# Layer 0's input projection in batches of four row blocks, with wider convolution taps

## The chip, the cores and the metric

The kernel runs on one core of a Trainium2 chip. The metric is the device time of one launch in microseconds (us); lower is better. The engines are named as in the profile: PE (TensorE, matrix products), ACT (ScalarE), DVE (VectorE), POOL (GpSimd), SP (SyncE, which issues the DMAs).

## The reference

A two-layer encoder over 256 tokens of width 2048, all in float32. Each layer first computes a modulation from a conditioning vector c and then one wide input projection, whose columns feed four kinds of mixers; an output projection with a gate and a gated feed-forward follow. What the change touches, for layer 0:

```python
mod = silu(c) @ w_mod + b_mod              # shift, scale, gate, ...: 2048 wide each
h = layernorm(x) * (1 + scale) + shift     # (256, 2048)
p = h @ w_in                               # one product, then cut by columns
a, g = p[:, AG]        # 1024 columns: GLU a * sigmoid(g), then a causal depthwise
                       # convolution of 31 taps over the tokens, norm, silu
u, v = p[:, UV]        # 512 + 512: gated MLP over tokens; v = gelu, normalised, mixed
q_lat, kv_lat, kr = p[:, B]   # 704: low-rank attention
sc = p[:, SC]          # 1024: short convolutions
gate = p[:, SB]        # 512: gate of that mixer
x = x + mod_gate * (concat(four mixers) @ w_out)
```

## The kernel before, in words

Tokens stay in SBUF; weights (and the modulation's weights) stream through once. `hF` holds the normalised x transposed: 16 row blocks ("kt") of 128 channels by 256 tokens, in four tiles. A *block* of PE work is one kt of 128 output columns: two float32 passes of 128x256 by the profile's count.

**Modulation.** For layer 0, `mod_block` (profile line L190) loads one 128x2048 piece of w_mod (1 MiB, tile `wmod`) and reduces it against c on DVE to one column. Two such pieces (shift, scale) make `first_mod_of(...).block(kt)`, which adds the bias (L1398) and modulates `hF[kt]`: on ACT for even kt (L116), on DVE for odd (L1404). Pieces for later stages, of L190 or of the accumulating form L200, are interleaved with the weights of B, C, and the output projection, so many MiB per load step as the table `RATES` says.

**The input projection of layer 0** is `by_pieces`. Its column groups are D (the GLU's 1024), U, V and E (u, v and gate; 512 each), then B (704) and C (1024). D accumulates in four PSUM banks over all 16 kt. U, V and E take turns in two banks each: the kt are cut into pieces `PIECES` of 1, 1, 2, 4, 4 and 4, and each piece's partial product is copied out by ACT (L1234, L1239) and added to a sum in SBUF by DVE (L1240). Within a piece a quarter of D's turns alternates with U, V and E.

For kt below `PLAIN_KT` = 4, and for U, V, E, B, C everywhere, products are plain float32 (weights in tile `wexact`, issued at L368). For D from kt 4 on, the weight (tile `wraw`, L373) is split: ACT rounds it (`whi`, L384), DVE subtracts (`wlo`, L385), `hF` is split in the same manner into `hT` (L403, L404), and PE makes three products of rounded operands in place of one plain product. Lines L113 and L116 are the helpers through which all products and all ACT activations go.

**Buffers.** `wraw` and `wmod` share four buffers of 1 MiB; `wexact` has eight of 512 KB, that it shares with `whi` and `wlo`. SP issues loads in the order of the code, and waits where a buffer is not free. `mods_for` decides how many modulation pieces are issued before a weight load: those that its kt needs, and further ones while the planner's PE clock is more than `LEAD_US` ahead of its DMA clock.

**After it.** `mix_d` makes the GLU and queues the convolution (`convD`, L824: one DVE operation for each of 31 taps and 4 column blocks) as background work, of which B and C run so many pieces after each load step as `STEPS` says. `mix_u`, `gelu_v` and `mix_v` finish u and v; `latent_group` makes B's latents; `group` makes C while `attend` interleaves attention's products (`ps_q`, `ps_kr`, `ps_qn`, `ps_kn`, `ps_v`, `ps_sc`, `ps_pT`, `ps_o`), whose results come out through ACT (`qg`, `rope`, `qn`, `kn`, `vv`, `p`) and DVE. `ps_mix` is the product that mixes the v tokens. The output projection follows (products `o`): its first chunk is 1024 columns in three rounded products, its chunks 1 and 2 are plain; then the feed-forward and layer 1.

**At the start** `normed_T` normalises x, transposes it on PE (`ps_xT`, L1377) and copies the eight results into `hF`: four on ACT (L1381), four on DVE (L1383). POOL takes the power that gives 1/std (L143), and one small DVE operation makes minus mean times 1/std (L559).

Of the kernel before, what the change touches and what calls it, by code (L numbers as in the profile page):

```python
# [7 lines left out]
F32 = mybir.dt.float32  # L8
# [5 lines left out]
P = 128  # L14
# [70 lines left out]
def encoder_kernel(ctx: ExitStack, tc: tile.TileContext, A: dict, consts: bass.AP, out: bass.AP):  # L85
# [687 lines left out]
    def mixers(l, w_in, Y, hF=None, first_mod=None):  # L773
# [44 lines left out]
        def conv_d(glu):  # L818
            yd = slot("convD").rearrange("p (j s) -> p j s", j=4)
            def tap(j, k):  # L820
                if k == 30:
                    ident_act(yd[:, j, :], glu[:, j, :], CW(30, j), CB(j))
                else:
                    dve.scalar_tensor_tensor(  # L824
                        out=yd[:, j, 30 - k :],
                        in0=glu[:, j, : S - 30 + k],
                        scalar=CW(k, j),
                        in1=yd[:, j, 30 - k :],
                        op0=ALU.mult,
                        op1=ALU.add,  # L830
                    )

            for j in range(4):
                for k in range(30, -1, -1):
                    background.append(lambda j=j, k=k: tap(j, k))
            background.append(lambda: norm_d(yd))

        def norm_d(yd):
# [330 lines left out]
                dve.tensor_tensor(out=c, in0=c, in1=t, op=ALU.mult)  # L1169

        if hF is not None:
            return by_pieces(l, w_in, hF, first_mod, mix_d, mix_u, gelu_v, mix_v, mix_b, mix_c, mix_e)
        phase(l, "V")
        first_group(w_in, C_UV + 512, gelu_v)
        phase(l, "D")
# [15 lines left out]
        run(group2(w_in, C_SB, f"E{l}", joined_e, bg=STEPS[l]["E"]))  # L1191
        drain_background()

    def by_pieces(l, w_in, hF, first_mod, mix_d, mix_u, gelu_v, mix_v, mix_b, mix_c, mix_e):


        hf = lambda kt: hF[kt // 4][:, kt % 4, :]
        accD = [acc_tile(f"D{l}_c{i}") for i in range(4)]
        hT[:] = [None] * (PLAIN_KT // 2) + [act_pair("hT") for _ in range((KT - PLAIN_KT) // 2)]
        sums = {}  # L1200
        for g in "UVE":
            both = actp.tile([P, 1024], F32, tag="act", name=f"sum{g}")
            sums[g] = [both[:, i * 512 : (i + 1) * 512] for i in range(2)]
        cols = {"U": C_UV, "V": C_UV + 512, "E": C_SB}

        def terms(kt, part):

            hi, lo = part
            if lo is None:
                return [(hi, hf(kt))]  # L1210
            xh, xl = (h[:, kt % 2, :] for h in hT[kt // 2][:2])
            return [(hi, xh), (hi, xl), (lo, xh)]

        def chan_major(ps, kt, part, blocks, first, last):
            ts = terms(kt, part)
            for i in blocks:
                o = ps[i // 2][:, (i % 2) * S : (i % 2 + 1) * S]
                for n, (w, x) in enumerate(ts):
                    mm(o, w[:, i * P : (i + 1) * P], x, first and n == 0 and i % 2 == 0, last and n == len(ts) - 1)

        def side(g, parts, k0, nkt):
            ps = [(ms_tile if g == "V" else acc_tile)(f"{g}{l}_{i}") for i in range(2)]
            for kt, part in parts:
                st, sp = kt == k0, kt == k0 + nkt - 1
                if g == "V":
                    ts = terms(kt, part)
                    for t in range(2):
                        for n, (w, x) in enumerate(ts):
                            mm(ps[t], x[:, t * P : (t + 1) * P], w, st and n == 0, sp and n == len(ts) - 1)
                else:  # L1230
                    chan_major(ps, kt, part, range(4), st, sp)
            for i in range(2):
                if k0 == 0:
                    act.copy(sums[g][i], ps[i])  # L1234
                elif k0 + nkt == KT:
                    dve.tensor_tensor(out=sums[g][i], in0=ps[i], in1=sums[g][i], op=ALU.add)
                else:
                    part = tmp_tile("part")
                    act.copy(part, ps[i])  # L1239
                    dve.tensor_tensor(out=sums[g][i], in0=part, in1=sums[g][i], op=ALU.add)  # L1240

        blocks = [lambda kt=kt, m=m: first_mod(kt, m) for kt in range(KT) for m in (SHIFT_M, SCALE_M)]
        fed = {"mods": 0, "dma": 0.0, "pe": 0.0}

        def feed(mb):
            fed["dma"] += mb * FEED_US
            fed["pe"] = max(fed["pe"], fed["dma"])

        def mods_for(kt):

            while fed["mods"] < len(blocks) and (
                fed["mods"] < 2 * (kt + 1) or fed["pe"] - fed["dma"] > LEAD_US
            ):
                blocks[fed["mods"]]()
                fed["mods"] += 1
                feed(1.0)
                if fed["mods"] == 8:
                    rest_of_constants()

        loaded = {}  # L1260

        def load(g, kt, nkt):

            if (g, kt) in loaded:
                return
            c0, width = (C_AG, 1024) if g == "D" else (cols[g], 512)
            nk = min(2048 // width, nkt)
            mods_for(kt + nk - 1)
            for j, p in enumerate(weights(w_in, kt, nk, c0, width, kt < PLAIN_KT or g != "D")):
                loaded[(g, kt + j)] = p  # L1270
            feed(nk * width / 2048)

        mods_for(0)
        for k0, nkt in PIECES:
            turns_d = [(kt, b) for kt in range(k0, k0 + nkt) for b in range(0, 8, 2)]
            for s in range(4):
                for kt, b in turns_d[s * nkt : (s + 1) * nkt]:
                    load("D", kt, nkt)
                    chan_major(accD, kt, loaded[("D", kt)], range(b, b + 2), kt == 0, kt == KT - 1)
                    fed["pe"] += 2 * BLOCK_US  # L1280
                if s < 3:
                    g = "UVE"[s]
                    load(g, k0, nkt)
                    side(g, [(kt, loaded[(g, kt)]) for kt in range(k0, k0 + nkt)], k0, nkt)
                    fed["pe"] += 4 * nkt * BLOCK_US
        mix_d(accD, None)
        mix_u(sums["U"], None)
        for t in range(2):
            gelu_v(t, sums["V"][t])
        mix_v()  # L1290
        phase(l, "B")
        run(latent_group(w_in, C_Q, f"B{l}", mix_b, hF=hf, bg=STEPS[l]["B"]))
        phase(l, "C")

        def mix_ce(cps, tps):
            mix_c(cps, tps)
            mix_e(sums["E"], None)

        run(group(w_in, C_SC, 1024, f"C{l}", mix_ce, hF=hf, bg=STEPS[l]["C"]))
        drain_background()  # L1300

# [60 lines left out]

    def normed_T(hF):

        rs = []
        for t in range(2):
            st = new_stats(f"in{t}")
            for c in range(4):
                dve.bn_stats(out=st[:, c, :], in_=X[t][:, c * 512 : (c + 1) * 512])
            rs.append(rstd_of(st, f"in{t}", True)[1])  # L1370
        for q in range(4):
            for t, r in enumerate(rs):
                xn = tmp_tile("xn")
                ident_act(xn, X[t][:, q * 512 : (q + 1) * 512], r[:, 0:1], r[:, 1:2])
                ps = ms_tile("ps_xT")
                for j in range(4):
                    pe.transpose(ps[:, j * P : (j + 1) * P], xn[:, j * P : (j + 1) * P], ident)  # L1377
                dst = hF[q][:, :, t * P : (t + 1) * P]
                src = ps.rearrange("p (j t) -> p j t", j=4)
                if t == 0:  # L1380
                    act.copy(dst, src)  # L1381
                else:
                    dve.tensor_copy(dst, src)  # L1383

    def first_mod_of(hF):

# [2 lines left out]
        def block(kt, m):  # L1389
# [8 lines left out]
            dve.tensor_tensor(out=both, in0=sums[kt], in1=bias, op=ALU.add)  # L1398
            sh, sc = both[:, 0:1], both[:, 1:2]
            h = hF[kt // 4][:, kt % 4, :]  # L1400
            if kt % 2 == 0:
                ident_act(h, h, sc, sh)
            else:
# [167 lines left out]
```

## Time and profile before

| | us |
|---|---|
| runs | 2271.78, 2269.24, 2270.52 |
| median | 2270.52 |
| the profiled execution | 2267.42 |
| its span in the trace | 2265.6 |
| up to the first product of D | 23.94 |
| input projection D, U, V, E | 161.35 |
| B | 40.89 |
| C with attention | 98.42 |
| output projection, chunk 0 / chunks 1 and 2 | 61.51 / 55.09 |
| the rest | 1824.40 |

The profiled execution is one launch on the chip; its span leaves out the 1.8 us around it. In rows of the trace, `D_c<-hT,whi` means a product into tile D_c from hT and whi; the times of matrix products are partly modelled, so starts are safer than durations. A wait row reads: engine, what it ran, what released it, then total us, times and the longest.

### The profile page before, as it was taken

What the parts mean: (1) busy time and instruction counts of PE and PEld (TensorE: products, weight loads), DVE (VectorE), ACT (ScalarE), POOL (GpSimd) and SP (SyncE); (2) the same over time, 40 slices, a digit from 0 to 9 for tenths busy, and PEclk for the clock granted to TensorE, in tenths of its full rate; (3) what the DMA queues carried; (4) which work ended last, traced back from release to release, by engine and by line L of the source; (5) the groups of instructions that cost most, each with busy time, mean ns of one, the idle gap of its engine ahead of it and who ended that gap; (6) DMA issues with size and microseconds to landing.
All of it is one profiled execution on the core that took longest, in us unless ns stands there. A gap on an engine that the chain in (4) does not pass through costs nothing. (4 is left out here: it accounts for less than half of the span.)

```text
span 2265.6 us, 28524 instructions
## 1 busy us (share of the span) xinstructions
PE 2198.8 (97%) x10948; PEld 1806.3 (80%) x10948; DVE 1769.3 (78%) x2347; ACT 1069.7 (47%) x1583; POOL 35.4 (2%) x38
## 2 busy tenths in 40 slices
PE   7789898999999999999999999999999999999997
PEld 5676776478888888888876888877888888888886
DVE  6868899588988888988968997877766565665776
ACT  3221231255555555544557544455545555554553
POOL 0000100000000000000000000000000000000000
PEclk9999999999999999999999999999999999999999
DMA  9889779769889889888865656776665555555554
GB/s 372 340 325 359 302 272 399 305 253 339 305 324 326 320 310 332 312 327 328 321 242 217 223 186 228 291 261 222 237 228 188 184 188 195 193 186 192 199 187 148
DMA packets 93315, 603.96 MB, mean 267 GB/s; under 512 B 10486, under 2 KB 10614, under 8 KB 27382
## 3 DMA queue, kind: packets, MB, share of 16 engines
q1 hardware_dynamic: 93178, 602.15, 72.8%
q8 instruction: 85, 1.39, 0.2%
q14 instruction: 52, 0.42, 0.1%
HBM read 600.01 MB, written 2.10 MB: 266 GB/s over the span
## 5 line engine op out<-in xcount | busy, mean ns | idle before, releaser
L384 ACT CAST whi<-wraw 128x1024 fp32r<-128x1024 f32 (+1 forms) x624 | 650.7, 1047 | 697.6 <-PE g_c L113 205.5
L385 DVE TENSOR_TENSOR wlo<-wraw,whi 128x1024 fp32r<-128x1024 f32 (+1 forms) x624 | 749.0, 1212 | 289.7 <-ACT whi L384 282.9
L113 PE MATMUL v_c<-hT,whi 128*128 128x512 f32 x1408 | 490.4, 392 | 0.0
L113 PE MATMUL g_c<-hT,whi 128*128 128x512 f32 x1280 | 444.9, 391 | 0.0
L113 PE MATMUL v_c<-hT,wlo 128*128 128x256 f32 x1408 | 394.5, 280 | 0.0
L113 PE MATMUL d<-whi,a 128*128 128x512 f32 x1344 | 386.1, 389 | 0.0
L113 PE MATMUL g_c<-hT,wlo 128*128 128x256 f32 x1280 | 358.4, 280 | 0.0
L113 PEld LDWEIGHTS v_c<-hT,whi 128*128 128x128 f32 x1408 | 263.4, 187 | 58.3
L190 DVE SCALAR_TENSOR_TENSOR wmod<-wmod,crep 128x2048 f32<-128x2048 f32 x128 | 291.4, 2284 | 12.6 <-DMA wmod<-in_w_mod_dram 12.6
L113 PEld LDWEIGHTS d<-whi,a 128*128 128x128 f32 x1344 | 252.2, 188 | 52.1
L113 PEld LDWEIGHTS g_c<-hT,whi 128*128 128x128 f32 x1280 | 239.4, 187 | 52.7
L113 PEld LDWEIGHTS v_c<-hT,wlo 128*128 128x128 f32 x1408 | 266.1, 189 | 0.2
L113 PEld LDWEIGHTS g_c<-hT,wlo 128*128 128x128 f32 x1280 | 241.9, 189 | 0.1
L113 PE MATMUL d<-wlo,a 128*128 128x512 f32 x672 | 232.9, 389 | 0.0
L200 DVE SCALAR_TENSOR_TENSOR macc<-wmod,cact,macc 128x2048 f32<-128x2048 f32 x60 | 140.8, 2347 | 18.0 <-DMA wmod<-in_w_mod_dram 17.8
L113 PEld LDWEIGHTS d<-wlo,a 128*128 128x128 f32 x672 | 126.2, 188 | 26.3
L113 PE MATMUL o<-whi,a 128*128 128x512 f32 x352 | 102.2, 397 | 4.5 <-ACT whi L384 4.5
L824 DVE SCALAR_TENSOR_TENSOR convD<-gluD,par,convD 128x251 f32<-128x251 f32 (+26 forms) x240 | 100.1, 464 | 0.7
L404 DVE TENSOR_TENSOR a<-g,a 128x512 fp32r<-128x512 f32 x132 | 88.6, 683 | 0.1
L528 PE MATMUL first<-wexact,hN 128*128 128x512 f32 x192 | 87.0, 603 | 1.5 <-ACT hN L116 1.2
L403 ACT CAST a<-g 128x512 fp32r<-128x512 f32 x132 | 81.1, 615 | 7.4 <-PE d L113 4.8
L113 PEld LDWEIGHTS o<-whi,a 128*128 128x128 f32 x352 | 67.0, 192 | 20.2 <-ACT whi L384 6.2
(326 smaller groups left out, 2390.3 us busy)
## 6 DMA issues: line engine op xcount, KB each, us to landing
wmod<-in_w_mod_dram SPq DMA_DIRECT2D x192, 1024.0 KB, 6.7
wraw<-in_ffn_w_up_dram SPq DMA_DIRECT2D x168, 1024.0 KB, 5.2
wraw<-in_ffn_w_down_dram SPq DMA_DIRECT2D x88, 1024.0 KB, 5.0
wraw<-in_w_in_dram SPq DMA_DIRECT2D x30, 1024.0 KB, 6.3
wexact<-in_w_in_dram SPq DMA_DIRECT2D x49, 512.0 KB, 7.2
wraw<-in_w_out_dram SPq DMA_DIRECT2D x24, 1024.0 KB, 5.6
wexact<-in_w_out_dram SPq DMA_DIRECT2D x16, 512.0 KB, 12.4
wexact<-in_ffn_w_up_dram SPq DMA_DIRECT2D x16, 512.0 KB, 7.9
```

The costliest lines, as they stand in the source:

```text
L113: pe.matmul(o, lhsT, rhs, start=start, stop=stop, skip_group_check=True)
L190: i = dve.scalar_tensor_tensor(out=raw, in0=raw, scalar=1.0, in1=crep, op0=ALU.mult, op1=ALU.mult, accum_out=col)
L200: i = dve.scalar_tensor_tensor(out=acc, in0=w, scalar=col, in1=acc, op0=ALU.mult, op1=ALU.add)
L384: held(act.copy(hi[:, :m], r), "cast")
L385: i = dve.tensor_tensor(out=lo[:, :m], in0=r, in1=hi[:, :m].bitcast(F32), op=ALU.subtract)
L403: act.copy(hi, src)
L404: dve.tensor_tensor(out=lo, in0=src, in1=hi.bitcast(F32), op=ALU.subtract)
L528: i = pe.matmul(ps, hN[kt // 4][:, kt % 4, t * P : (t + 1) * P], parts[kt], start=kt == 0, stop=kt == KT - 1, skip_group_check=True,)
L824: dve.scalar_tensor_tensor(out=yd[:, j, 30 - k :], in0=glu[:, j, : S - 30 + k], scalar=CW(k, j), in1=yd[:, j, 30 - k :], op0=ALU.mult, op1 ...
```

## The change

`by_blocks` replaces `by_pieces`. The kt are cut into four batches of four. D (four banks) and U (two) accumulate in banks of their own from kt 0 to 15; V and E share two banks in turn within each batch, ACT copies each batch's partial sum out (`keep_part`), and DVE adds them up after the last batch (`total`). All products are plain float32. The planner of modulation loads counts DMA, DVE and PE and runs ahead by `LEAD_US`. In `normed_T` all eight copies and the minus-mean product are on ACT; all of `hF`'s modulation too. The convolution's tap k of layer 0 becomes four ACT scalings into a tile `scaled` (four buffers) and one DVE addition over 128x4x~255; eight empty background pieces follow tap 23. `mix_v` is postponed into B. `RATES` of layer 0 give C 2.4 and out 1.6 MiB a step, `STEPS` fewer pieces.

```diff
-    dict(B=1.2, C=2.1, out=1.8, up=0.7, down=0.7),
+    dict(B=1.2, C=2.4, out=1.6, up=0.7, down=0.7),
...
-    dict(B=7, C=8, up=2),
+    dict(B=1, C=4, up=2),
...
-PIECES = ((0, 1), (1, 1), (2, 2), (4, 4), (8, 4), (12, 4))
-FEED_US, BLOCK_US, LEAD_US = 2.7, 0.43, 6.0
-PLAIN_KT = 4
+BATCHES = ((0, 4), (4, 4), (8, 4), (12, 4))
+FEED_US, BLOCK_US, LEAD_US = 2.7, 0.432, 6.0
...
+            scaled = []
+            def taps(k):
+                if k == 30:
+                    for j in range(4):
+                        tap(j, k)
+                    return
+                if len(scaled) < 4:
+                    scaled.append(actp.tile([P, 1024], F32, tag="act", name="scaled").rearrange("p (j s) -> p j s", j=4))
+                t, n = scaled[(29 - k) % 4], S - 30 + k
+                for j in range(4):
+                    act.activation(out=t[:, j, :n], in_=glu[:, j, :n], func=AF.Copy, scale=CW(k, j))
+                dve.tensor_tensor(out=yd[:, :, 30 - k :], in0=yd[:, :, 30 - k :], in1=t[:, :, :n], op=ALU.add)
-            for j in range(4):
+            if hF is not None:
                 for k in range(30, -1, -1):
-                    background.append(lambda j=j, k=k: tap(j, k))
+                    background.append(lambda k=k: taps(k))
+                    if k == 23:
+                        background.extend([lambda: None] * 8)
...
+        accU = [acc_tile(f"U{l}_c{i}") for i in range(2)]
+        parts = {"V": [], "E": []}
+        at = {"mods": 0, "dma": 10.0, "dve": 15.0, "pe": 0.0}
+        def mods_for(kt):
+            while at["mods"] < len(blocks) and (
+                at["mods"] < 2 * (kt + 1) or at["pe"] - at["dma"] > LEAD_US
+            ):
+                blocks[at["mods"]]()
+                at["dma"] += FEED_US
+                at["dve"] = max(at["dve"], at["dma"] + 1.6) + 2.4
+                ready[at["mods"] // 2] = at["dve"] + 1.0
...
+        for k0, nkt in BATCHES:
+            accV = [ms_tile(f"V{l}_{t}") for t in range(2)]
+            for kt in range(k0, k0 + nkt):
+                d, uv = load(kt, 1, C_AG, 1024)[0], load(kt, 1, C_UV, 1024)[0]
...
+                for product in (product_v, product_du) if kt == k0 + nkt - 1 else (product_du, product_v):
+                    product()
+            keep_part("V", accV)
+            if k0 + nkt == KT:
+                mix_d(accD, None)
+                mix_u(accU, None)
+                for t, v in enumerate(total("V")):
+                    gelu_v(t, v)
+            es = []
+            for kt in range(k0, k0 + nkt, 2):
+                es.extend(load(kt, 2, C_SB, 512))
+            accE = [ms_tile(f"E{l}_{i}") for i in range(2)]
+            for kt, w in enumerate(es, k0):
+                channels(accE, kt, w, kt == k0, kt == k0 + nkt - 1)
+            keep_part("E", accE)
+        sumE = total("E")
+        postponed.append(mix_v)
...
-                src = ps.rearrange("p (j t) -> p j t", j=4)
-                if t == 0:
-                    act.copy(dst, src)
-                else:
-                    dve.tensor_copy(dst, src)
+                act.copy(dst, ps.rearrange("p (j t) -> p j t", j=4))
...
-            if kt % 2 == 0:
-                ident_act(h, h, sc, sh)
-            else:
-                dve.tensor_scalar(out=h, in0=h, scalar1=sc, scalar2=sh, op0=ALU.mult, op1=ALU.add)
-                if kt >= PLAIN_KT:
-                    split(hT[kt // 2], hF[kt // 4][:, kt % 4 - 1 : kt % 4 + 1, :])
+            ident_act(h, h, sc, sh)
```

How the work stands in the engines' rows (the changed kernel's lines lie some lower or higher than those of before: L111 for L113, L366 for L368, L187 for L189).

SP before, where the loads of kt 4 to 7 begin: `wmod` is a piece of modulation, `wexact` a plain weight, `wraw` a weight of D that is split.

```order
L368 DMA wexact<-in_w_in_dram 128x1024 x4
L189 DMA wmod<-in_w_mod_dram 128x2048 x2
L368 DMA wexact<-in_w_in_dram 128x1024
L189 DMA wmod<-in_w_mod_dram 128x2048 x2
L373 DMA wraw<-in_w_in_dram 128x2048
L189 DMA wmod<-in_w_mod_dram 128x2048 x4
L368 DMA wexact<-in_w_in_dram 128x1024 x2
L189 DMA wmod<-in_w_mod_dram 128x2048 x2
L368 DMA wexact<-in_w_in_dram 128x1024 x2
```

SP of the changed kernel in the same place, from the first load of a batch:

```order
L366 DMA wexact<-in_w_in_dram 128x1024 x2
L187 DMA wmod<-in_w_mod_dram 128x2048
L366 DMA wexact<-in_w_in_dram 128x1024
L187 DMA wmod<-in_w_mod_dram 128x2048
L366 DMA wexact<-in_w_in_dram 128x1024
L187 DMA wmod<-in_w_mod_dram 128x2048
L366 DMA wexact<-in_w_in_dram 128x1024
L187 DMA wmod<-in_w_mod_dram 128x2048
L366 DMA wexact<-in_w_in_dram 128x1024
L187 DMA wmod<-in_w_mod_dram 128x2048
```

One modulation piece now stands ahead of nearly each weight, in place of two to four at a time.

PE of the changed kernel at the end of a batch (D_c and U_c hold two blocks of columns each, `hF_116` is the tile of kt 4 to 7):

```order
L111 MATMUL D_c_209<-hF_116,wexact 128x256 x2
L111 MATMUL D_c_210<-hF_116,wexact 128x256 x2
L111 MATMUL V_0_370<-wexact,hF_116 128x512
L111 MATMUL V_1_371<-wexact,hF_116 128x512
L111 MATMUL U_c_211<-hF_116,wexact 128x256 x2
L111 MATMUL U_c_212<-hF_116,wexact 128x256 x2
L111 MATMUL E_0_491<-hF_116,wexact 128x256 x2
L111 MATMUL E_1_492<-hF_116,wexact 128x256 x2
```

Between V's last product and E's first, which takes the same banks, stand U's four blocks.

ACT before, from the scaling of the queries (`qg`) to the values (`vv`) in C:

```order
L988 ACTIVATE qg<-ps_q,par 128x256
L991 ACTIVATE qg<-ps_q,par 128x256
L988 ACTIVATE qg<-ps_q,par 128x256
L1007 COPY rope<-ps_kr 64x256
L1008 COPY rope<-ps_kr 64x256
L1017 COPY qn<-ps_qn 128x512 x2
L1042 COPY kn<-ps_kn 128x512 x2
L1049 COPY vv<-ps_v 128x512 x2
```

ACT of the changed kernel, from the same place to the second `qn`:

```order
L1006 ACTIVATE qg<-ps_q,par 128x256
L842 ACTIVATE scaled<-gluD,par 128x235 x2
L842 ACTIVATE scaled<-gluD,par 128x234 x3
L1025 COPY rope<-ps_kr 64x256
L1026 COPY rope<-ps_kr 64x256
L842 ACTIVATE scaled<-gluD,par 128x234
L842 ACTIVATE scaled<-gluD,par 128x233 x4
L842 ACTIVATE scaled<-gluD,par 128x232 x3
L1035 COPY qn<-ps_qn 128x512
L842 ACTIVATE scaled<-gluD,par 128x232
L842 ACTIVATE scaled<-gluD,par 128x231 x4
L842 ACTIVATE scaled<-gluD,par 128x230
```

Three to eight scalings of the taps now stand between one copy of attention and the next.

More of the change, by code (lines that the diff above doesn't have):

```diff
@@ L1171, in mixers @@
         if hF is not None:
[L1172 removed]
+            return by_blocks(l, w_in, hF, first_mod, mix_d, mix_u, gelu_v, mix_v, mix_b, mix_c, mix_e)
         phase(l, "V")
@@ L1192, in mixers, with by_blocks @@
         drain_background()
-    def by_pieces(l, w_in, hF, first_mod, mix_d, mix_u, gelu_v, mix_v, mix_b, mix_c, mix_e):
+    def by_blocks(l, w_in, hF, first_mod, mix_d, mix_u, gelu_v, mix_v, mix_b, mix_c, mix_e):
         hf = lambda kt: hF[kt // 4][:, kt % 4, :]
         accD = [acc_tile(f"D{l}_c{i}") for i in range(4)]
[L1199 to L1216, printed above, removed]
-                o = ps[i // 2][:, (i % 2) * S : (i % 2 + 1) * S]
[L1218 to L1226, printed above, removed]
-                    for t in range(2):
-                        for n, (w, x) in enumerate(ts):
-                            mm(ps[t], x[:, t * P : (t + 1) * P], w, st and n == 0, sp and n == len(ts) - 1)
-                else:
[L1231 to L1236, printed above, removed]
-                else:
[L1238 to L1290, printed above, removed]
@@ new lines, in by_blocks @@
+        accU = [acc_tile(f"U{l}_c{i}") for i in range(2)]
+        parts = {"V": [], "E": []}
+        blocks = [lambda kt=kt, m=m: first_mod(kt, m) for kt in range(KT) for m in (SHIFT_M, SCALE_M)]
+        at = {"mods": 0, "dma": 10.0, "dve": 15.0, "pe": 0.0}
+        ready = {}
+        def mods_for(kt):
[6 more added lines that the diff above has]
+                ready[at["mods"] // 2] = at["dve"] + 1.0
+                at["mods"] += 1
+                if at["mods"] == 8:
+                    rest_of_constants()
@@ new lines, in load, with channels @@
+        def load(kt, nk, c0, width):
+            mods_for(kt + nk - 1)
+            got = weights(w_in, kt, nk, c0, width, True)
+            at["dma"] += FEED_US * nk * width / 2048
+            at["pe"] = max(at["pe"], at["dma"] + 1.6, ready[kt + nk - 1]) + nk * width / P * BLOCK_US
+            return [w for w, _ in got]
+        def channels(ps, kt, w, start, stop):
+            for i in range(w.shape[1] // P):
+                o = ps[i // 2][:, (i % 2) * S : (i % 2 + 1) * S]
+                mm(o, w[:, i * P : (i + 1) * P], hf(kt), start and i % 2 == 0, stop)
@@ new lines, in keep_part, with total @@
+        def keep_part(g, ps):
+            if len(parts[g]) < len(BATCHES) - 1:
+                both = actp.tile([P, 1024], F32, tag="act", name=f"part{g}")
+                for i in range(2):
+                    act.copy(both[:, i * 512 : (i + 1) * 512], ps[i])
+                parts[g].append(both)
+            else:
+                parts[g].append(ps)
+        def total(g):
+            *sums, ps = parts[g]
+            for other in sums[1:]:
+                dve.tensor_tensor(out=sums[0], in0=sums[0], in1=other, op=ALU.add)
+            halves = [sums[0][:, i * 512 : (i + 1) * 512] for i in range(2)]
+            for i in range(2):
+                dve.tensor_tensor(out=halves[i], in0=ps[i], in1=halves[i], op=ALU.add)
+            return halves
@@ L1296, in mix_ce @@
             mix_c(cps, tps)
-            mix_e(sums["E"], None)
+            mix_e(sumE, None)
         run(group(w_in, C_SC, 1024, f"C{l}", mix_ce, hF=hf, bg=STEPS[l]["C"]))
```

23 lines of the change are left out of this document (18 added, 5 removed).

## The prediction

> **What bounds the kernel now.** I read the page's head first, then a table of stretches that I cut at the first product of each stage, then what TensorE (PE) waits for in those that the change touches.
>
> ```profile
> span 2265.6 us, 28524 instructions
> PE 2198.8 (97%) x10948; PEld 1806.3 (80%) x10948; DVE 1769.3 (78%) x2347; ACT 1069.7 (47%) x1583; POOL 35.4 (2%) x38
> ```
>
> PE is busy 97% of the span, so only PE work, PE waits and PE's clock can move the end. Stretches, with span, busy time (count) by engine, granted clock, DMA share and GB/s: input projection, latents (B), C with attention, output projection chunk 0, its chunks 1 and 2, the rest.
>
> ```profile
> 23.94:185.29 161.35, 141.03 (x672) 113.42 (x673) 114.38 (x137) 38.95 (x57) 0.31 (x1) 0.96 0.88 345
> 185.29:226.18 40.89, 39.92 (x146) 26.03 (x145) 38.88 (x68) 8.82 (x19) 1.91 (x2) 1.00 0.97 361
> 226.18:324.60 98.42, 92.23 (x429) 76.68 (x428) 91.16 (x155) 24.91 (x58) 11.03 (x4) 0.97 0.77 290
> 324.60:386.11 61.51, 50.03 (x197) 37.87 (x196) 56.90 (x69) 19.74 (x26) 1.70 (x1) 0.94 0.93 365
> 386.11:441.20 55.09, 55.09 (x129) 24.12 (x127) 34.86 (x54) 5.81 (x16) 1.17 (x2) 1.00 0.93 380
> 441.20:2265.60 1824.40, 1805.22 (x9342) 1519.57 (x9342) 1420.41 (x1844) 959.01 (x1392) 17.68 (x20) 1.00 0.69 248
> ```
>
> The first stretch is where the slack is: PE is idle 161.35 − 141.03 = 20.3 us, at a mean clock of 0.96. Its waits add up to the same 20.3 (us in total, times, longest):
>
> ```profile
> PE D_c L113 <- ACT whi L384: 11.6, 5, 4.2
> PE D_c L113 <- DVE wlo L385: 4.7, 3, 2.9
> PE D_c L113 <- ACT hF L116: 3.0, 1, 3.0
> PE U L113 <- DMA wexact<-in_w_in_dram: 0.7, 1, 0.7
> PE V L113 <- DMA wexact<-in_w_in_dram: 0.3, 1, 0.3
> ```
>
> 16.3 of it is the D group waiting for the rounded half of its weights (ACT's cast) or the remainder (DVE's subtraction). Two prices of a block (128 rows by 128 columns by 256 tokens) follow from PE's timeline (start, us, count): plain float32 in 16 blocks of C at full clock, and three-product blocks of D, one every 0.36 us.
>
> ```profile
> 282.13 7.07 PE L113 MATMUL C_c<-hF,wexact 128*128 128x256 f32 x32
> 289.04 0.60 PE L1097 MATMUL ps_pT<-cst,p 128*128 128x128 f32 x4
> ...
> 73.12 0.40 PE L113 MATMUL D_c<-hT,whi 128*128 128x256 f32 x2
> ...
> 73.48 0.40 PE L113 MATMUL D_c<-hT,whi 128*128 128x256 f32 x2
> ...
> 45.00 3.20 PE L113 MATMUL D_c<-hF,wexact 128*128 128x256 f32 x8 [2.96 <-ACT hF L116]
> 47.99 1.33 PE L113 MATMUL U<-hF,wexact 128*128 128x256 f32 x3
> ```
>
> (289.04 − 282.13)/16 = 0.432 us a plain block. The last two rows are the same kind of work right after a wait of 2.96 us: 4 blocks take 47.99 − 45.00 = 2.99 us, 0.75 each. After a wait PE runs slow for some microseconds. The stage at full clock is 224 × 0.432 + 96 × 0.36 = 131.3 us; with 20.3 of waits 151.6; the other 9.7 us of the 161.35 are this slow clock.
>
> **The change, part by part.** *Stage 1.* All 320 blocks become plain: 320 × 0.432 = 138.2 us, 6.9 more work. In return no product waits for a cast or a remainder, so 16.3 us of waits go with most of their slow clock. The start moves a little: ACT takes four more transposed copies and four tiny operations before the first product, against DVE's four.
>
> ```profile
> L1383 DVE COPY hF<-ps_xT 128x512 f32<-128x512 f32 x4 | 2.8, 689 | 2.9 <-PE ps_xT L1377 2.9
> L1239 ACT COPY part<-V 128x512 f32<-128x512 f32 x8 | 4.7, 585 | 13.1 <-PE V L113 13.1
> L190 DVE SCALAR_TENSOR_TENSOR wmod<-wmod,crep 128x2048 f32<-128x2048 f32 x47 | 106.7, 2284 | 1.5 <-DMA wmod<-in_w_mod_dram 1.5
> L385 DVE TENSOR_TENSOR wlo<-wraw,whi 128x1024 fp32r<-128x1024 f32 x18 | 21.5, 1218 | 0.8 <-ACT whi L384 0.8
> ```
>
> The copies (585 ns on ACT) lie mostly beside transposes; I take 24.3 for the first product (bounds 23.94 and 26.3, all four in series). Without a wait the stage then ends at 24.3 + 138.2 = **162.5** instead of 185.29: **−22.8 us**.
>
> What is late next? First the transfers. One batch of four row blocks takes 8 MiB of modulation, 2 of D, 2 of U with V, 1 of E: 13 MiB, and the stage about 55 with what is loaded before its first product. Saturated stretches of the trace (same columns) move 411 and 418 GB/s:
>
> ```profile
> 20.00:40.00 20.00, 19.24 (x77) 14.88 (x77) 10.68 (x15) 8.94 (x15) 0.00 (x0) 1.00 1.01 411
> 80.00:100.00 20.00, 15.16 (x55) 9.92 (x54) 17.31 (x22) 6.17 (x9) 0.00 (x0) 0.92 1.02 418
> ```
>
> 411 is 2.55 us a MiB, 33.2 a batch, against 80 × 0.432 = 34.6 us of PE. I walked the new issue list (every load waits for its buffer, 8 of weights and 4 of modulation) at this pace: row block 1 lands at 28.4 for a start at 31.2, block 2 at 36.1 for 38.1; the tightest modulation is block 7's, ready at 76.9 for 79.6; nothing waits, and the transfers end at 144. The margin is thin: up to 2.65 us a MiB nothing waits, at 2.75 the stage ends at 167.6, at 2.93 (358 GB/s) at 177.2, at 3.04 (345, the stage's mean row, which PE's waits held down) at 183.0.
>
> A rule speaks against it. The Trainium skill, "DMA: Bandwidth & Descriptors", section "Where 436 GB/s comes from", states that for transfers from HBM to SBUF the HBM side, about 358 GB/s a core, binds; by it the stage would end near 177 and the whole gain 15 us less. The 411 and 418 rows are such transfers over 20 us and disagree, so I keep 2.55.
>
> Second, DVE: 32 modulation blocks × 2.28 = 73 us, with small sums and late additions some 85 of 138, covered. Third, the two banks that V and E share: E follows V under only 4 blocks of U (1.7 us) while ACT copies V's banks (2 × 0.585 = 1.2); V follows E under 12 blocks (5.2). Nothing, or 0.3 a batch at worst. The partial sums are added at the end, beside E's 16 blocks and B's; the last batch's E waits until V's are added (4 additions, some 3.8 us, under 11 blocks, 4.75).
>
> *B, C and attention.* PE's waits there now, and in chunk 0:
>
> ```profile
> PE ps_q L982 <- ACT qg L988: 5.9, 1, 5.9
> PE ps_mix L113 <- DVE rs_A L556: 1.0, 1, 1.0
> ...
> PE o L113 <- DVE wlo L385: 6.9, 5, 4.7
> PE o L113 <- ACT whi L384: 4.5, 4, 1.5
> ```
>
> The taps change engine. Rows of a tap on DVE now and of the ACT operation nearest to the new scaling, then the C stretch's groups of taps and of modulation for later stages (busy us, mean ns):
>
> ```profile
> 211.53 5.85 DVE L824 SCALAR_TENSOR_TENSOR convD<-gluD,par,convD 128x245 f32<-128x245 f32 x15
> ...
> 330.70 1.69 ACT L1145 ACTIVATE yc<-chC,par 128x256 f32<-128x256 f32 x4
> ...
> L824 DVE SCALAR_TENSOR_TENSOR convD<-gluD,par,convD 128x228 f32<-128x228 f32 (+24 forms) x77 | 32.3, 457 | 0.4
> L200 DVE SCALAR_TENSOR_TENSOR macc<-wmod,cact,macc 128x2048 f32<-128x2048 f32 x8 | 18.8, 2346 | 0.0
> ```
>
> Four DVE taps (4 × 0.39 = 1.56 us) become four ACT scalings (4 × 0.42 = 1.7) and one DVE addition (about 1.2, by the remainder's row). In the C stretch DVE, busy 91.16 of 98.42, loses 77 old taps (32 us), and gets some 13 wide ones (15.6) and 2.4 more modulation blocks (2.4 × 2.35 = 5.6): 11 us lighter. ACT gets some 50 scalings, 21 us on 24.91 of 98.42. By volume both fit, and B keeps its load: 17 to 20 wide additions (20 to 24 us) where 43 of the 120 taps (43 × 0.457 = 20 us) stood. What V still has to have normalised moves from the stage's end behind B's first unit, beside B's products. But in C the scalings stand in the engines' rows among attention's own operations (qg, qn, kn, vv, p), and each of attention's hand-offs to PE is covered by at most some C blocks. I take: the wait for qg 5.9 → 3.5, one small wait of 1 more there, B's mix 1.0 → 2, softmax's transposes +4.4 from two or three runs of four scalings (1.7 each) ahead of a hand-off. Sum **+4** (bounds −6, the 5.9 gone and nothing new, and +20, one run of scalings and an addition, 2.9, ahead of each of seven hand-offs).
>
> *Chunk 0.* Per weight tile the planner now fetches 1.6 instead of 1.8 MiB of modulation beside its 1.0. Over 8 tiles that is 1.6 MiB and as many DVE blocks less: 1.6 × 2.5 = 4.0 us, out of 11.4 us of waits of which about 5 belong to the first tiles, that are not changed. **−3.5** (bounds 0 and −6.5).
>
> *The rest* keeps its order: 0 (±2). **Sum** −22.8 + 4 − 3.5 = −22.3. The profiled execution took 2267.4 us (span 2265.6 and 1.8 around it): 2245.1. The median of the three runs, 2270.5, is 3.1 above it: **2248 us**.
>
> **The rivals.** *Transfers pace the stage.* For it: the margin of 4% and the 345 of the stage now. Against it: the saturated stretches, over 410. At 358 GB/s the stage ends 14.7 later: 2263; at 2.8 us a MiB it ends at 170.7: 2256.
>
> *Attention is stretched*: at 10 to 20 us instead of 4, 2254 to 2264. *On the other side*: the scalings and additions that stand among attention's operations all in series with its chain, 50 × 0.42 + 13 × 1.2 = 36.6 us, 32.6 more than I take: **2281**. It decides from 22.3 + 4 = 26 us on. Against it: a C block can stand beside each step, and 92.23 of 98.42 are busy now with DVE nearly full; for it: ACT had almost nothing there, and its row is served in order.
>
> *The change doesn't do what it says*: modulations aren't ahead, since the four modulation buffers come free only as DVE reads them, and PE waits 1 to 2 us a batch with its slow clock: 4 to 8 us, 2254. *Better*: C no worse and chunk 0 cleared: 2238.
>
> **How the numbers follow.** Forecast 0.60 (2240 to 2257 on its own bounds), transfers 0.12, attention stretched 0.12, slower 0.06, modulations late 0.05, better 0.05. The range 2238 to 2265 leaves out the slower case, and the tails of transfers and attention. A measurement of this kernel tells about 0.2% (4.5 us) from no change: faster means below 2266. That is the forecast, better, late modulations and nearly all of the transfers' and the stretched case: 0.89; same 0.05; slower 0.06.
>
> **What would show it.** In the changed kernel's stretches: first product near 24.3; the stage some 138 us long with under 2 us of waits, clock 1.00 and about 400 GB/s until 144; no product of D, U, V or E waiting for a DMA or for the modulated hF. If instead such waits add up to 10 us and the DMA row reads 360 or less all along, the transfers' rival holds. C with its attention should stay within 98 + 4; waits of ps_q, ps_kr, ps_pT or ps_o for ACT or DVE with scaled or convD ahead of it show the stretch. Chunk 0 should be 58 instead of 61.5. After 441 − 22 the same rows should stand as before.

## The result, and the profile after

The changed kernel takes 2245.6 us (median of four runs, 2243.6 to 2246.6) against 2271.2 for the kernel before: a ratio of 0.9878, 95% interval 0.985 to 0.9907. The forecast was 2248, in a range of 2238 to 2265. On another chip the same two gave 2244.6 and 2271.5, ratio 0.9888 (0.9873 to 0.9903).

The table of stretches of the changed kernel, cut at the same events as before (span; busy time of PE, PE's weight loads, DVE, ACT and POOL with counts; granted clock, DMA share, GB/s): before the first product, input projection, B, C up to its last product, output projection chunk 0 with the wait ahead of it, chunks 1 and 2, the rest.

```profile
0.00:25.10 25.10, 15.69 (x41) 8.34 (x41) 15.31 (x24) 14.83 (x26) 3.62 (x10) 1.00 0.91 364
25.10:165.10 140.00, 140.00 (x577) 110.92 (x577) 76.65 (x89) 26.55 (x47) 1.37 (x3) 1.00 0.99 395
165.10:204.80 39.70, 39.70 (x146) 26.13 (x146) 38.87 (x35) 25.67 (x65) 0.00 (x0) 1.00 0.95 364
204.80:304.20 99.40, 94.41 (x431) 77.35 (x429) 78.37 (x97) 45.38 (x114) 3.13 (x4) 0.97 0.73 282
304.20:365.10 60.90, 48.16 (x192) 36.55 (x193) 57.47 (x63) 20.59 (x26) 0.00 (x0) 0.97 0.92 364
365.10:420.20 55.10, 55.10 (x131) 24.34 (x131) 35.52 (x58) 6.89 (x18) 1.55 (x2) 1.00 0.95 385
420.20:2241.80 1821.60, 1803.15 (x9343) 1518.21 (x9341) 1420.52 (x1843) 957.45 (x1391) 19.47 (x19) 1.00 0.70 249
```

The input projection is busy 140.00 of 140.00 us at a clock of 1.00: its 20.3 us of waits and its slow clock are gone. Against before: the start +1.2, the input projection −21.4, B −1.2, C +1.0, chunk 0 −0.6, chunks 1 and 2 the same, the rest −2.8: −23.8 in the profiled executions. PE's waits from C's first product to chunk 0's last are as large as before; the five largest (us, times, longest):

```profile
PE o L111 <- ACT whi L382: 7.6, 4, 3.6
PE o L111 <- DVE wlo L383: 5.1, 6, 2.6
PE ps_q L1000 <- ACT qg L1006: 3.2, 1, 3.2
PE ps_qn L111 <- DVE kvr L1017: 0.6, 1, 0.6
PE ps_pT L1115 <- DVE p L1106: 0.4, 1, 0.4
```

One caution for all that follows. From the first product of the feed-forward (`first`) on, all kernels here have the same products, yet profiles of them differ: from there to the first down product they took 500.4 to 501.6 us in nine profiles and 505.7 to 509.8 in five, with at most 1.0 us of waits and a clock of 1.00, and from there to the end 1820.0 to 1837.4. So an edit is read from the stretches it touches and from the start of `first`: 444.4 before, 421.8 in the changed kernel (422.9 in a second profile). One whole time alone tells apart only what is larger than that 17 us. The stretches wander too: the input projection of the kernel before took 161.4 us in one profile and 163.1 in another kernel that has it unchanged.

### The profile page after: what moved, and what is told of

Same layout as the page of the kernel before. It is cut to its first block, busy times and chain, and to the rows that moved or that the text cites. A ratio compares the mean times of both kernels' runs of the same rounds, so it can differ in the third digit from the quotient of the medians.

```text
span 2241.8 us, 28321 instructions
## 1 busy us (share of the span) xinstructions
PE 2196.2 (98%) x10852; PEld 1801.8 (80%) x10852; DVE 1722.7 (77%) x2203; ACT 1097.4 (49%) x1683; POOL 29.2 (1%) x38
## 5 line engine op out<-in xcount | busy, mean ns | idle before, releaser
L382 ACT CAST whi<-wraw 128x1024 fp32r<-128x1024 f32 (+1 forms) x612 | 638.0, 1046 | 693.0 <-PE g_c L111 208.1
L383 DVE TENSOR_TENSOR wlo<-wraw,whi 128x1024 fp32r<-128x1024 f32 (+1 forms) x612 | 736.0, 1215 | 287.0 <-ACT whi L382 280.5
L111 PE MATMUL v_c<-hT,whi 128*128 128x512 f32 x1408 | 490.4, 392 | 0.0
L111 PE MATMUL g_c<-hT,whi 128*128 128x512 f32 x1280 | 444.9, 391 | 0.0
L111 PE MATMUL v_c<-hT,wlo 128*128 128x256 f32 x1408 | 394.6, 280 | 0.0
L111 PE MATMUL d<-whi,a 128*128 128x512 f32 x1344 | 386.3, 389 | 0.0
L111 PE MATMUL g_c<-hT,wlo 128*128 128x256 f32 x1280 | 358.4, 280 | 0.0
L111 PEld LDWEIGHTS v_c<-hT,whi 128*128 128x128 f32 x1408 | 263.4, 187 | 58.3
L111 PEld LDWEIGHTS d<-whi,a 128*128 128x128 f32 x1344 | 252.1, 188 | 52.4
L111 PEld LDWEIGHTS g_c<-hT,whi 128*128 128x128 f32 x1280 | 239.4, 187 | 52.7
L111 PEld LDWEIGHTS v_c<-hT,wlo 128*128 128x128 f32 x1408 | 266.1, 189 | 0.2
L111 PEld LDWEIGHTS g_c<-hT,wlo 128*128 128x128 f32 x1280 | 241.9, 189 | 0.1
L111 PE MATMUL d<-wlo,a 128*128 128x512 f32 x672 | 232.8, 389 | 0.0
L111 PEld LDWEIGHTS d<-wlo,a 128*128 128x128 f32 x672 | 126.1, 188 | 26.2
L111 PE MATMUL o<-whi,a 128*128 128x512 f32 x352 | 100.9, 395 | 7.6 <-ACT whi L382 7.6
L111 PEld LDWEIGHTS o<-whi,a 128*128 128x128 f32 x352 | 66.5, 190 | 23.2 <-ACT whi L382 9.3
L1353 DVE SCALAR_TENSOR_TENSOR u<-g,par,u 128x254 f32<-128x254 f32 (+1 forms) x176 | 74.3, 480 | 0.4 <-ACT u L114 0.2
## 6 DMA issues: line engine op xcount, KB each, us to landing
wexact<-in_w_out_dram SPq DMA_DIRECT2D x16, 512.0 KB, 12.9
```

What stands on the lines that cost most here:

```text
L111: pe.matmul(o, lhsT, rhs, start=start, stop=stop, skip_group_check=True)
L382: held(act.copy(hi[:, :m], r), "cast")
L383: i = dve.tensor_tensor(out=lo[:, :m], in0=r, in1=hi[:, :m].bitcast(F32), op=ALU.subtract)
L1353: dve.scalar_tensor_tensor(out=u[:, sh:], in0=x[:, : S - sh], scalar=col(k, j), in1=u[:, sh:], op0=ALU.mult, op1=ALU.add)
```

## The experiments

**The split or the batches?** Theory: the stage gained because no product waits for ACT's cast or DVE's remainder. Rival: the gain is that of the batches, in which D and U hold their banks and the loads come evenly. Two kernels, each with one half of the change. First the kernel before with D plain throughout:

```diff
-PLAIN_KT = 4
+PLAIN_KT = 16
```

> The kernel before with all of D in plain float32 and nothing else changed: pieces, side groups and partial sums stay. If the gain of the stage comes from products that no longer wait for a cast or a remainder, the stage (161.4 us before, 140.0 in the changed kernel) should be 143 to 149 here: 138.2 of work, the 4.0 us of other waits that the stage of before has, and 1 to 6 of slow clock; no wait for whi or wlo in it; the whole about 2252. If it comes from the batches and from D and U holding their banks, so that the partial sums through ACT and DVE are what cost, the stage should stay at 154 or more and the whole at 2260 or more.

```profile
23.90:172.40 148.50, 142.89 (x576) 112.43 (x577) 96.47 (x119) 22.36 (x38) 0.31 (x1) 0.98 0.94 376
```

Then the changed kernel with D split, in the new order:

```diff
-            got = weights(w_in, kt, nk, c0, width, True)
+            got = weights(w_in, kt, nk, c0, width, c0 != C_AG or kt < 4)
...
+                mm(o, hi[:, b], xh, False, False)
+                mm(o, hi[:, b], xl, False, False)
+                mm(o, lo[:, b], xh, False, stop)
...
             ident_act(h, h, sc, sh)
+            if kt >= 4 and kt % 2 == 1:
+                split(hT[kt // 2], hF[kt // 4][:, kt % 4 - 1 : kt % 4 + 1, :])
```

> The changed kernel with D split again from row block 4 on (ACT's cast, DVE's subtraction, three rounded products), in the new order and banks; V's and E's partial sums are added as they come, to have room for the split activations. If the waits for casts and remainders are what the change removed, they come back: 10 to 16 us of waits for whi or wlo, clock below 0.98, and the stage 12 to 22 us longer than the changed kernel's 140.0 less 6.9 of work, so 145 to 157. If batches and banks are the cause, the waits stay under 3 us, and the stage is 133 to 139, shorter than the changed kernel's, since three rounded products take 0.36 us and a plain one 0.432.

Its stretch, and D's waits in it:

```profile
25.10:169.30 144.20, 136.98 (x674) 111.19 (x674) 97.20 (x114) 41.68 (x65) 1.95 (x3) 0.98 0.96 379
```

```profile
PE D_c L111 <- ACT whi L382: 6.0, 3, 2.8
...
PE D_c L111 <- DVE wlo L383: 1.2, 3, 0.4
```

| us | D split | D plain |
|---|---|---|
| input projection, pieces as before | 161.4 | 148.5 |
| input projection, batches as changed | 144.2 | 140.0 |
| start of `first`, kernel before | 444.4 | 432.5 |
| start of `first`, changed kernel | 420.1 | 421.8 |

The first kernel did what the theory says (148.5, and 2256.0 on the whole, ratio 0.9923, 0.9896 to 0.9951). The second fell between the two: 144.2 is just below the theory's 145, and its 7.2 us of waits for the split lie between the theory's 10 and the rival's 3. So each half alone brings more than half of the stage's gain: plain products 12.9 us, batches with the split kept 17.2, both 21.4. The theory by itself is too narrow. Of the 16.3 us of waits for casts and remainders, 9 go when the loads and banks are arranged in batches, with every cast still made. What in the batches does it was not taken apart further; this kernel also modulates on ACT alone, as the changed one does, and adds its partial sums as they come. With split D the batches do 6.9 us less work than plain, and lose 7.2 of waits and the slow clock behind them (0.98): plain products are worth 4.2 there.

At the start of `first` even that is not seen. The kernel with D split is there at 420.1, ahead of the changed one (421.8 and 422.9). What it loses in the stage comes back in C, 95.9 us for 99.4, and from there to `first`, 115.2 for 117.6:

```profile
209.00:304.90 95.90, 93.42 (x431) 77.35 (x429) 77.20 (x97) 44.31 (x111) 2.33 (x4) 0.96 0.79 300
304.90:420.10 115.20, 104.38 (x331) 62.39 (x329) 92.42 (x121) 29.74 (x49) 1.55 (x2) 0.96 0.94 373
```

On the whole it takes 2253.9, a ratio to before of 0.9886 (0.9833 to 0.9939), beside 0.9878 and 0.9888 for the changed kernel. So plain products bring 11.9 us up to `first` in the old pieces; with the batches no run shows a gain from them beyond the stage itself. Why C is shorter with D split stays open: the partial sums that are added early and D's weights in loads of 1 MiB came with it, and no run separates them.

**Is it the modulation loaded ahead?**

```diff
-FEED_US, BLOCK_US, LEAD_US = 2.7, 0.432, 6.0
+FEED_US, BLOCK_US, LEAD_US = 2.7, 0.432, 1e9
```

> The changed kernel without the lead: modulation pieces are issued only ahead of the first weights that need them. By a walk of the issue list at 2.55 us a MiB nothing waits either way: stage 140 (139 to 142), whole within 2 us of the changed kernel's 2243.6. If the lead carries the change, PE waits for the modulated hF at most row blocks, 4 us or more in the stage, with a clock below 0.99.

```profile
25.10:165.10 140.00, 139.42 (x577) 109.98 (x577) 76.61 (x89) 26.69 (x47) 1.38 (x3) 1.00 0.98 394
```

No. Stage 140.0, the whole 2244.7 (one run): the lead is worth nothing that can be seen. The pieces of modulation that each row block needs come early enough.

**How thin is the transfers' slack?** Half a MiB more per row block, read by nobody; this is the only edit. The extra tile also takes its turn in the buffers of the plain weights.

```diff
             got = weights(w_in, kt, nk, c0, width, True)
+            if c0 == C_UV:
+                tag = ("whi", "wlo")[exact_turn[0] % 2]
+                exact_turn[0] += 1
+                r = splitp.tile([P, 1024], F32, tag=tag, name="extra")
+                end = w_in[0].size - kt * P * 1024
+                nc.sync.dma_start(out=r, in_=w_in[0].flat[end - P * 1024 : end].rearrange("(p c) -> p c", p=P))
```

> The changed kernel with half a MiB more loaded behind every row block's U and V weights, which nothing reads: 15 in place of 13 MiB a batch (38.3 us at 2.55 us a MiB against 34.6 of products). If the slack of the transfers is as thin as I worked out, PE waits for wexact or for the modulated hF from the first batch on, and the stage takes 11 to 22 us more than 140.0 (walked: 13.7 at 2.55 us a MiB, 10.7 at 2.5, 19.7 at 2.65, without the slow clock behind the waits). If the transfers have more room than the rows of before show (2.4 us a MiB or less), it takes under 8 us more. The DMA row should read 405 GB/s or more throughout; 360 would speak for a limit there.

The stage's row, and its only group of waits:

```profile
25.10:175.00 149.90, 143.24 (x577) 110.95 (x577) 79.00 (x92) 26.88 (x47) 1.37 (x3) 0.99 1.02 414
```

```profile
PE D_c L111 <- ACT hF L114: 6.7, 3, 2.7
```

9.9 us more, at 414 GB/s over 150 us. That is just short of the 11 I gave, and above the 8 of the rival: the slack is about as thin as worked out. The three waits for the modulated hF end at 85.4, 123.3 and 161.1 us, ahead of the last row block (7, 11 and 15) of the second, third and fourth batch; block 7 is the one whose modulation the prediction had as the tightest. None is for a weight. The whole took 2261.9 (one run). In the changed kernel itself the transfers run at the same pace in the stage's middle and PE waits for nothing:

```profile
40.00:80.00 40.00, 40.00 (x169) 31.74 (x168) 22.51 (x27) 5.14 (x9) 0.00 (x0) 1.00 1.02 415
80.00:120.00 40.00, 40.00 (x167) 31.47 (x166) 20.87 (x22) 4.74 (x8) 0.00 (x0) 1.00 1.00 407
```

**The taps.** The old narrow taps in the changed kernel:

```diff
-    dict(B=1, C=4, up=2),
+    dict(B=7, C=8, up=2),
...
-            if hF is not None:
-                for k in range(30, -1, -1):
-                    background.append(lambda k=k: taps(k))
...
+            for j in range(4):
+                for k in range(30, -1, -1):
+                    background.append(lambda j=j, k=k: tap(j, k))
```

> The changed kernel with the convolution as before (each tap one DVE operation, 7 and 8 background pieces a load step, no empty ones). Stage 140.0 as in the changed kernel. If the wide taps are what lets C take the 2.4 more modulation blocks, DVE, some 11 us fuller, holds the end of the convolution and attention's hand-offs: from C's first product to chunk 0's last 165 to 172 us against 160.3 in the changed kernel. If the scalings in ACT's row are what stretches C (99.4 us against 98.4 before), it is shorter without them: 155 to 159.

From C's first product to chunk 0's last, and the largest wait ahead of chunk 0:

```profile
203.60:365.90 162.30, 143.14 (x623) 113.88 (x622) 144.41 (x213) 45.81 (x84) 9.22 (x4) 0.96 0.80 308
```

```profile
PE ps_q L994 <- ACT qg L1000: 5.4, 1, 5.4
```

162.3 against 160.3 in the changed kernel: neither 165 nor 159. The wide taps take 8.6 us off DVE (144.4 to 135.9) and put 20 on ACT, and PE's wait for qg is 3.2 with them and 5.4 without. The scalings do not stretch attention; what the taps bring up to the feed-forward is under 2 us (its start 422.5 against 421.8 and 422.9). The whole took 2258.0 in its one run, nearly all of the difference behind `first` (1833.8 us from there to the end, against 1820.0). Without the eight empty pieces:

```diff
-                    if k == 23:
-                        background.extend([lambda: None] * 8)
```

> The changed kernel without the eight empty background pieces: the taps end two load steps sooner. If the late convolution is what holds the first cast of chunk 0 (ACT's row had the convolution's last operations ahead of it, 3.6 us of PE's wait), that wait falls under 1.5 us and C with chunk 0 takes 157 to 159 against 160.3. If the empty pieces keep the taps out of attention's way, the wait for qg (3.2) grows by 2 us or more, and C with chunk 0 takes 160 or longer.

```profile
204.60:364.00 159.40, 143.06 (x623) 114.29 (x622) 135.75 (x159) 66.12 (x139) 3.13 (x4) 0.96 0.81 311
```

0.9 us shorter, the first wait for a cast 4.7 in place of 3.6, the wait for qg the same 3.2. Neither side's mechanism shows; the empty pieces decide nothing (whole 2243.1, one run).

**The rates.** The old ones in the changed kernel, twice:

```diff
-    dict(B=1.2, C=2.4, out=1.6, up=0.7, down=0.7),
+    dict(B=1.2, C=2.1, out=1.8, up=0.7, down=0.7),
```

> The changed kernel with the rates of before (2.1 MiB of modulation a load step in C, 1.8 in the output projection). If the amount of modulation beside chunk 0's tiles sets its waits, as I predicted (3.5 us), chunk 0 with its first wait goes from 60.9 to 63 to 66 us and its waits from 12.7 to 15 or more; C gets shorter by 0 to 2. If the order at the end of C and the buffers set them, chunk 0 stays within 2 us and its waits within 1.5.

> The changed kernel with the old rates (2.1 and 1.8 MiB a load step) once more. In its first profile chunk 0 took 10.6 us longer, 2.2 of it waits and the rest slow clock. If that holds, the feed-forward starts at 428 to 434 again and the whole is 6 to 12 us over the changed kernel's on this chip. If the slow clock was that execution's alone, it starts at 423 to 427 and the whole is 2 to 5 us over.

C with chunk 0 in the first profile (whole row), and in the second, chunk 0 and C apart:

```profile
204.50:375.40 170.90, 150.85 (x624) 120.18 (x623) 136.10 (x161) 65.85 (x139) 3.13 (x4) 0.91 0.80 303
```

```profile
302.00:366.10 64.10, 50.77 (x195) 37.98 (x194) 60.68 (x70) 21.77 (x28) 0.53 (x1) 0.92 0.86 340
204.50:302.00 97.50, 93.37 (x430) 77.32 (x428) 74.01 (x89) 43.98 (x112) 2.60 (x4) 0.96 0.76 287
```

The first profile seemed to say 10.6 us (whole 2261.2, one run). It was that execution's: PE was busy 8.3 us longer with the same products at a clock of 0.91. In the second the two stretches take 161.6 together, and those of the changed kernel on the same chip 161.7; the feed-forward starts at 422.8 and 422.9; the wholes are 2246.7 and 2244.6. That is the edge of the second branch (a start of 423 to 427, the whole 2 to 5 over). The new rates move some 2 us from chunk 0 into C. The same in the kernel before:

```diff
-    dict(B=1.2, C=2.1, out=1.8, up=0.7, down=0.7),
+    dict(B=1.2, C=2.4, out=1.6, up=0.7, down=0.7),
```

> The kernel before with the new rates alone (2.4 MiB of modulation a load step in C, 1.6 in the output projection). If the rates are worth what I took for chunk 0 wherever they stand, chunk 0 falls from 61.5 to 57 to 59.5 us, C grows by 0 to 2, since DVE is busy 91 of 98 us there already, and the whole is 1 to 4 us faster than before. If C's full DVE is what then holds the end of C, C grows by 4 us or more and the whole is not faster.

```profile
227.90:325.20 97.30, 91.26 (x414) 74.99 (x413) 89.53 (x152) 20.51 (x52) 10.11 (x3) 0.96 0.78 295
325.20:388.60 63.40, 52.94 (x211) 39.94 (x211) 57.40 (x69) 24.13 (x32) 0.70 (x1) 0.92 0.90 342
```

Chunk 0 did not fall to 57 to 59.5, it took 63.4; its waits were 10.0 us for 11.4, but the clock 0.92 for 0.94. C did not grow; ratio 0.9996 (0.9982 to 1.001). Both expectations missed: no gain from the rates shows in either kernel.

**A version meant to be faster.** Chunk 0 of layer 0's output projection in plain float32 as well:

```diff
-            plain=(1024, 1536) if l == 0 else (),
+            plain=(0, 1024, 1536) if l == 0 else (),
```

> The changed kernel with chunk 0 of layer 0's output projection in plain float32 too: 128 blocks, 55.3 us at 0.432, in place of 46.1 of work and 12.7 us of waits with a slow clock (60.9 with the first wait). If its waits are again those of products for a cast or a remainder, they go, and chunk 0 takes 55.5 to 57: 4 to 5 us less on the whole. If transfers pace it (2.6 MiB a tile, 6.6 us at 2.55 us a MiB, against 6.9 of products), waits for DMA take their place and it takes 60 or more.

```profile
303.80:358.78 54.98, 54.98 (x130) 24.34 (x130) 36.92 (x42) 2.89 (x7) 0.00 (x0) 1.00 0.95 384
```

No wait is left, as the first expectation had it, and the time is a little under its 55.5: 54.98 us busy out of 54.98, clock 1.00, for 60.9. DVE is busy 36.9 us of it where it was 57.5 of 60.9. The feed-forward starts at 414.9; the whole is 2245.9 (2237.9 to 2251.2), a ratio to before of 0.9857 (0.9824 to 0.9891). Together with four of the first copies back on DVE:

```diff
-                act.copy(dst, ps.rearrange("p (j t) -> p j t", j=4))
+                src = ps.rearrange("p (j t) -> p j t", j=4)
+                if t == 0:
+                    act.copy(dst, src)
+                else:
+                    dve.tensor_copy(dst, src)
```

> The changed kernel with chunk 0 of layer 0's output projection in plain float32, and four of the eight first copies back on DVE. Chunk 0 took 55.0 us without a wait in the run with that edit alone, and the first product should start at 24 to 24.6 in place of 25.1: the feed-forward starts at 413.5 to 415 and the whole is 6 to 9 us below the changed kernel's on this chip. If the copies on DVE hold the first modulation instead, the start stays at 25 or the first batch waits for hF.

> The changed kernel once more, unchanged, beside the next three on one chip. Its first products of the feed-forward started at 421.8 us in its first profile; the same program should give 420 to 424, and whole times that wander with the stretch behind that point (1808 to 1826 us in the runs so far, with the same instructions).

The feed-forward starts at 416.1, in the changed kernel on that chip at 422.9; 413.5 to 415 was expected. The copies brought nothing: the first product stays at 25.1. On the whole 2241.8 against 2244.6 (ratios to before 0.9867, 0.9845 to 0.9888, and 0.9888, 0.9873 to 0.9903). The intervals overlap: that the whole is faster than the changed kernel is not shown. This kernel's profile had the longer feed-forward of the caution above (508.1 to the first down product, against 500.6); its fastest run, 2236.4, and the changed kernel's, 2243.2, are as far apart as the starts, but that compares one run of four on each side.

## Why the prediction was right, step by step

- **The stage.** Forecast −22.8 at its end; measured −20.2 (185.3 to 165.1). No wait and full clock, as forecast. The first product came at 25.1 instead of 24.3, and 1.8 us lie over 138.2, a term that the sum did not have: the first sixteen products of D take 5.5 us where the next sixteen take 3.45 (one lasts up to 796 ns, 379 as a rule). The profile's clock reads 1.00 there, so a slow clock is not shown to be the reason. The step's reason was half of it: I gave the whole gain to the products that wait no more for casts. The two halves alone show that the batches remove 9 of the 16.3 us of those waits with the casts kept, and that with them the plain products are worth 4.2 us in the stage and nothing that shows at `first`. So the end of the stage came out near the forecast although its cause was only half seen.
- **The transfers.** "Nothing waits" held. The rival, a pace of 358 GB/s, fell: 407 and 415 GB/s over 40 us each, and 414 over 150 with the extra loads. The rule of the Trainium skill that was weighed ("DMA: Bandwidth & Descriptors", section "Where 436 GB/s comes from", HBM binding at about 358 GB/s a core) is contradicted by these rows, taken with the kernel on one core.
- **B, C, attention.** Forecast +4, measured −0.2 (B −1.2, C +1.0). The wait for qg went from 5.9 to 3.2 (I took 3.5), but B's mix waited for nothing, in place of my 2, and the softmax's transposes 0.4, in place of 4.4. The scalings that stand in ACT's row among attention's copies cost next to nothing: this step over-priced them.
- **Chunk 0.** Forecast −3.5, measured −0.6, its waits 12.7 with the one ahead of it, 11.4 before. This step failed: less modulation beside the tiles did not shorten chunk 0 in the kernel before (63.4 us for 61.5), and in the changed one it only moved 2 us into C. DVE is busy 57.5 of 60.9 us, 31.8 of it with modulation and 19.0 with remainders; taking the remainders and casts away cleared the stretch.
- **The rest.** Forecast 0, measured −2.8. 1.6 of it lies ahead of the first product of the feed-forward, which starts 1.6 us behind the cut instead of 3.2; the wait for xn there is 0.6 us where it was 1.5. The errors +2.6, −4.2, +2.9 and −2.8 almost cancel: −22.3 forecast, −23.8 measured. That the sum is so close is luck; that most of it is the stage is not.

The slower rival (scalings in series with attention) did not occur, nor the late modulations.

## What to carry to other kernels

When a product waits for work that another engine does on its operand, price both cures: the dearer product that needs no such work (here 0.432 us for 0.36), and an even order of loads with fixed accumulators. They overlap: alone they brought 12.9 and 17.2 of the stage's 21.4 us, and at `first` the kernel with the second alone was not behind the one with both. Which part of the batches does it was not taken apart. Moving modulation loads from one stretch to the next moved 2 us with them and gained nothing. What did clear a stretch was taking remainders off the engine that was full there: chunk 0, with DVE busy 57.5 of 60.9 us and PE waiting, went to 55.0 with plain products.

## What the runs showed of the hardware

**POOL takes longer beside DVE.** The first product is 1.2 us late, and not by the copies: with four of them back on DVE the transposes from the second tile on still stand 1.2 us later than before (the first of them at 16.69 for 15.51). POOL's power for the second tile's 1/std, before and in the changed kernel, with what DVE runs at that time in the latter:

```profile
13.86 0.55 POOL L143 TENSOR_TENSOR rs_in<-rs_in,mhalf 128x1 f32<-128x1 f32 x1 [3.14 <-DVE rs_in L556]
```

```profile
12.82 2.56 POOL L141 TENSOR_TENSOR rs_in<-rs_in,mhalf 128x1 f32<-128x1 f32 x1 [2.24 <-DVE rs_in L554]
...
12.68 2.29 DVE L188 SCALAR_TENSOR_TENSOR wmod<-wmod,crep 128x2048 f32<-128x2048 f32 x1
...
15.41 0.29 ACT L1385 ACTIVATE rs_in<-rs_in 128x1 f32<-128x1 f32 x1 [1.14 <-POOL rs_in L141]
```

Before, DVE itself needed the result for minus mean times 1/std, and so stood still while POOL worked: 0.55 us. With that product on ACT, DVE goes on to a piece of modulation, the power takes 2.56 us beside it, and ACT waits 1.14 for it. The Trainium skill, "GPSIMD Engine Reference", section "1. Specifications", states that POOL's SBUF interfaces are shared with VectorE, with contention for DVE instructions with two SBUF inputs, as this one has; the two rows agree. No run here put only the product back on DVE, so that the power makes the 1.2 us is read from the rows, not shown by a run.

**The same rounded products at two paces.** In the feed-forward's gate products, over 80 us of each profile (560 to 640), the changed kernel and the combined one on the same chip:

```profile
L111 PE MATMUL g_c<-hT,whi 128*128 128x512 f32 x128 | 44.6, 392 | 0.0
```

```profile
L111 PE MATMUL g_c<-hT,whi 128*128 128x512 f32 x128 | 45.3, 398 | 0.0
```

That is 1.5% on this group, at a granted clock of 1.00 in both and with no wait. Kept up over the 500 us to the first down product it would be 7.5 us, an estimate from these two rows, and the second profile is 7.5 us longer there (508.1 for 500.6). What sets it stays open.
